# Reordering the last two heads, and moving small transposes and loads, in a hybrid decoder layer on one Trainium2 core

## The chip, the cores and the metric

The kernel runs on one core of one Trainium2 chip. A core has a matrix engine (TensorE: PE in the profile, PEld for its weight loads), VectorE (DVE), ScalarE (ACT), GpSimd (POOL) and SyncE (SP, whose queue issues most DMAs). Each engine executes its own instructions in order and waits on semaphores for the others. The metric is the device time of one execution in microseconds.

## The reference

One layer of a decoder over 2048 prompt positions of width 1024, and one new position for each of 8 sample rows with 512 positions of paged cache behind them. All arrays are float32.

```python
h = rms_norm(x, g_norm); p = h @ w_in            # 1024 -> 3592
q, k, v, fz, za, u, gv, zc = split(p)            # 8 heads x 64; 4 groups x 128
q, k = rms_norm(q, g_q), rms_norm(k, g_k)        # per head
c = cumsum(log_sigmoid(fz + b_f))
s[t, s'] = q_t . k_s' * 64**-0.5 + c_t - c_s'    # causal
attn = softmax(s) @ v
mix = tril(w_s) @ rms_norm(gv) + b_s             # in chunks of 128 positions
y = x + concat(attn * silu(za), u * mix * silu(zc)) @ w_out
```

The sample rows do the same, with keys, values and forget values of their cache pages in front. Outputs are y, k, v and the log forget values for both, and the normalised gv of the sample rows.

## The kernel before

Float32 products are made of parts: an operand is split into a high part and a remainder (`split`: ScalarE or GpSimd writes the high part, VectorE subtracts), and the projections add three matmuls (high by high, high by low, low by high).

The work has three stages.

*First stage (to about 585 us).* `order` goes through eight units of input columns. Units 3, 0, 1, 2 (q, k, v, fz) and 4 (gv) run over the 16 token tiles; units 5, 6 (u, zc) and 7 (za) run by features over the first two of four 512-token chunks. `load_unit` loads the next unit's eight weight tiles through three `raw` buffers and splits them. `sample_products` (helper lines 412, 413 copy its result out) makes a unit's product for the 8 sample rows, in a PSUM bank of the same four (`acc`) in the gv unit; it stands ahead of token tile 14. Results go to DRAM scratch (`qk_hi`, `qk_lo`, `v_st`, `mixT`, `zT`).

*Second stage (to about 1150 us).* `UNITS` lists pairs (head, chunk of 512 queries). For each, `values(at)` runs over key tiles of 128: two score matmuls into a `sc` bank, ScalarE's exp into `p` (L1036; a ring of ten), GpSimd's running sum `acc` of p for the row sums (L1043, L1045), and p times v into the `av` bank in groups of eight. Scores are shifted by each query's extreme score, which `maxima` finds beforehand with one rougher matmul into `tp` banks (three) and reductions on VectorE (L970, L972, L983); a transpose and a copy (L991) bring it into a row (`shifts`), stored to `mrow`, and `load_queries` loads queries and shift together. The maxima run ahead of the attention by `AHEAD` of a head, head after head. `load_head` loads a head's keys for the maxima (`k2`), keys for the scores (`k1`) and values, a piece every `LSTEP`.

At the end of a unit, L1057 and L1058 copy the result to `at`, which goes to `aT` in DRAM; `add_up` transposes `acc`, sums it (L1066) and takes the reciprocal (L1067); `done` transposes that, and L1073 copies it to a row stored in `rT`. After each odd head's chunk, `gate` loads the pair's 128 rows of z (`zT`), a (`aT`) and r (`rT`, spread over partitions), multiplies z by r on GpSimd (L1133) and that by a on VectorE (L1134), and stores `gm`.

The remaining two chunks of u, zc and za are the `filler`: matmuls into one bank (`fl`) that `fill` puts between the attention's, in proportion to `FILL`, `FILL0` (first chunk of a head) or `FILL7` (the last units). When it is used up, the out weights are loaded and split (`load_out_weights`, L1114, L271) and the out tiles follow as filler, if their inputs are there. The sample rows' gating and attention (`decode_gate`, `decode_attention`) are spread over the stage from head 1 on; L718 is a prefix sum on VectorE.

*Third stage.* The out tiles that are left: 16 tiles of 128 tokens, two halves of 512 columns (`out_products`), added to x and stored.

TensorE's order is the program's own. Its clock `Pe.clock` is counted by hand in ns of matmul work; `later(ns, fn)` puts off a piece of work by so much TensorE work, and what is so given is not issued ahead of TensorE's latest matmul at that place. So the constants (`SLAG`, `STLAG`, `GTLAG`, `OLAG`, `FGAP` and so on) are distances in TensorE work. The other engines' order is the scheduler's, within these bounds. SBUF tiles of 512 columns rotate through 11 buffers (`wk`), those of 2048 through 16.

Of the kernel before, what the change touches and what calls it, by code (L numbers as in the profile page):

```python
# [9 lines left out]
F32 = mybir.dt.float32  # L10
# [4 lines left out]
ALU = mybir.AluOpType  # L15
# [4 lines left out]
P = 128  # L20
# [4 lines left out]
NH = 8  # L25
# [15 lines left out]
WOLAG = 9000.0  # L41
WOSTEP = 1500.0
OLAG = 9000.0
GTLAG = 8000.0
STLAG = 5000.0
STLAST = 2500.0
SLAG = 3000.0
# [5 lines left out]
FGAP = 1500.0  # L53
# [7 lines left out]
VPARTS = 7  # L61
QLEAD = 10
PRE = 1.2
DEC = (3300, 15000, 26000, 14000)
# [4 lines left out]
WOENG = ('act',)  # L69
# [15 lines left out]
def hymba_step(ctx, tc, x_prompt, x_sample, cache_k, cache_v, cache_logf, page_table, g_norm, w_in,  # L85
# [615 lines left out]
    def decode_attention():  # L701
# [16 lines left out]
        nc.vector.tensor_tensor_scan(cc, one, lfT, 0.0, op0=ALU.mult, op1=ALU.add)  # L718
# [23 lines left out]
        for b in range(B):  # L742
            hs = slice(b * NH, (b + 1) * NH)
            vb = s8(t="vb").rearrange("p (g f) -> p g f", g=NPG)
            page_loads(b, range(NPG), [(cv, lambda g: vb[:, g])])
# [12 lines left out]
            yield DEC[2]  # L758
# [114 lines left out]
    def load_head(h):  # L873
# [24 lines left out]
        return [lambda: keys(0), rows_of, lambda: keys(1)], [  # L898
# [43 lines left out]
    def maxima(hd):  # L942

        h = hd["h"]
        nxt = qhi.pop() if qhi else load_hi(h, 0)
        for c in range(2):
            q = nxt
            for i in range(8 * c, 8 * c + 8, 2):
                if i == 2:
                    nxt = load_hi(h, 1)  # L950
                if i == 10 and h + 1 < NH:
                    qhi.append(load_hi(h + 1, 0))
                if i % 4 == 0:
                    part = sm.tile([P, 4, i // 4 + 1], F32, tag="mn", bufs=3, name=tname("mn"))
                cuts = [pieces((j + 1) * P) for j in (i, i + 1)]
                ends = []
                for j, cut in zip((i, i + 1), (cuts[0], cuts[1][::-1])):
                    for (c0, m) in cut:
                        n = cuts[j - i].index((c0, m))
                        end = n == len(cut) - 1  # L960
                        sp = bank("tp")[:, :m]
                        mm(sp, q[:HD + 2, (j % 8) * P:(j % 8 + 1) * P], hd["k2"][:HD + 2, c0:c0 + m], True, not end,
                           max(m, 256) * 0.422)
                        if end:
                            ends.append((sp, m, j, n))
                            if j > i:
                                for (sp, m_, _, _) in ends:
                                    mm(sp[:, m_ - P:], identb, maskb[:, 0], False, True, 56)
                                for (sp, _, j_, n_) in ends:
                                    nc.vector.tensor_reduce(part[:, j_ % 4, n_:n_ + 1], sp, axis=AX.X, op=ALU.min)  # L970
                        else:
                            nc.vector.tensor_reduce(part[:, j % 4, n:n + 1], sp, axis=AX.X, op=ALU.min)  # L972
                        yield m * 0.422
                if i % 4 == 2:
                    shifts(h, i // 4, part)

    shifted = set()
    qhi = []
# [19 lines left out]

    avq = []
# [13 lines left out]
    def values(at):  # L1013
# [3 lines left out]
        for kt in range(4 * c + 4):  # L1017
            if kt == 1 and c == 0 and h < NH - 1:
                Pe.loads += chain(*load_head(h + 1))
                Pe.load_at = Pe.clock + LHEAD  # L1020
            if at + 1 < len(UNITS) and UNITS[at + 1] not in qload and kt >= 4 * c + 4 - (
                    QLEAD if UNITS[at + 1] in shifted else 4):
                qload[UNITS[at + 1]] = load_queries(*UNITS[at + 1])
# [23 lines left out]
            def step(kt=kt, p=p, n0=n0, acc=acc, c=c, st=st, at=at):  # L1047
# [7 lines left out]
                if fin:  # L1055
                    t = s2(t="at")
# [4 lines left out]
                    def add_up():  # L1061
# [7 lines left out]
                        def done():  # L1069
# [5 lines left out]
                            def store():  # L1075
                                nc.sync.dma_start(rT[h, c * 512:(c + 1) * 512].rearrange("(n p) -> n p", p=P), t)
                                if h % 2:
                                    later(STLAST, lambda: gate(h // 2, c))
# [304 lines left out]
```

## Time and profile before

| | |
|---|---|
| runs of the kernel | 1331.54, 1327.94, 1326.21 us; median 1327.94 |
| the profiled execution | 1326.85 us, span 1325.0 us, mean granted TensorE clock 0.992 |
| TensorE busy | 97% of the span, 6544 matmuls |
| VectorE, ScalarE, GpSimd busy | 49%, 33%, 42% |
| DMA | 201 MB, mean 152 GB/s |

Times in the profile are microseconds from the span's start. A line such as `PE tp L200 <- DVE sm L1067: 4.1, 3, 2.0` says that TensorE's instructions of line 200 that write `tp` waited 4.1 us in all, three times, 2.0 at most, and that the last thing they waited for was the VectorE instruction of line 1067 that writes `sm`. A helper's instructions all have the helper's line: 196 is any matmul, 200 any transpose. A timeline row has start, duration, engine, line, operation and tiles, shapes, count, and in brackets the engine's idle time before it and what ended it. Matmuls are pipelined: a busy TensorE can still be slowed by a lower clock, which the table of stretches shows as granted clock.

### The profile page before, as it was taken

To read this page: it belongs to the slowest core of one execution; us is meant where nothing else is said; L and a number is where in the kernel's file an instruction comes from. 1 tells how busy PE (TensorE), PEld (TensorE's weight loads), DVE (VectorE), ACT (ScalarE), POOL (GpSimd) and SP (SyncE) were. 2 spreads that over 40 slices of the span, in tenths; PEclk is the share of its full clock that TensorE was granted. 3 is DMA by queue.
4 is the path that set the end of the run, shared out by engine and by line. 5 is a ranking of instruction groups with operands and counts; after the bars stand their busy time and mean duration, and the time that the engine had idled before them with its cause. 6 is when DMAs were issued, how large, how long until landed. Compare 5 with 4: busy or idle time off the path is not lost.

```text
span 1325.0 us, 19322 instructions
## 1 busy us (share of the span) xinstructions
PE 1289.8 (97%) x6544; PEld 1005.7 (76%) x6544; DVE 646.6 (49%) x1216; ACT 432.1 (33%) x781; POOL 559.0 (42%) x587
## 2 busy tenths in 40 slices
PE   6999999999999999999999999999999999999998
PEld 5999999999888777866666666666656565788877
DVE  4445654534667643354476544454444566322321
ACT  5542332222222111114444444444444556300100
POOL 3113343322222555305656566566656759600000
PEclk9999999999999999999999999999999999999999
DMA  6644353555213868945436584576464545773221
GB/s 220 186 121 116 89 139 113 150 144 144 81 46 81 289 209 278 290 137 137 103 85 172 158 211 123 149 221 181 131 181 128 153 132 181 200 264 116 96 81 48
DMA packets 189028, 201.43 MB, mean 152 GB/s; under 512 B 40002, under 2 KB 138626, under 8 KB 188906
## 3 DMA queue, kind: packets, MB, share of 16 engines
q1 hardware_dynamic: 185042, 191.43, 50.5%
q10 hardware_dynamic: 3488, 8.39, 1.6%
q8 instruction: 52, 0.85, 0.3%
q14 instruction: 46, 0.38, 0.1%
q0 software_dynamic: 400, 0.38, 0.1%
HBM read 127.43 MB, written 72.73 MB: 151 GB/s over the span
## 4 chain that ended last, share of the span: by engine, by line
PE 90%; DVE 3%; DMA 2%; issue 2%; ACT 1%; POOL 1%; SPq 1%; DVEq 0%; POOLq 0%; ACTq 0%
PE acc L196 36%; PE sc L196 22%; PE fl L196 10%; PE av L196 9%; PE tp L196 6%; PE tp L200 4%; PE pm L196 3%; DMA xp<-in_x_prompt_dram 1%; DMA q<-qk_hi 1%; POOL acc L1045 0%; DMA g<-gm 0%; ACT p L1036 0%; SPq L326 0%; DVE wl L279 0%; DVE mn L972 0%
## 5 line engine op out<-in xcount | busy, mean ns | idle before, releaser
L1045 POOL TENSOR_TENSOR acc<-acc,p 128x512 f32<-128x512 f32 (+3 forms) x256 | 287.8, 1124 | 79.7 <-ACT p L1036 64.3
L1036 ACT ACTIVATE p<-sc,zero 128x512 f32<-128x512 f32 (+1 forms) x320 | 194.8, 623 | 177.3 <-PE sc L196 166.7
L196 PE MATMUL acc<-wh,hh 128*128 128x384 f32 (+2 forms) x640 | 229.0, 358 | 0.0
L196 PE MATMUL acc<-wl,hh 128*128 128x384 f32 (+2 forms) x640 | 223.3, 349 | 1.2 <-DVE wl L279 1.2
L196 PE MATMUL acc<-wh,hl 128*128 128x384 f32 (+2 forms) x640 | 223.0, 348 | 0.6 <-DVE hl L271 0.6
L196 PE MATMUL sc<-q,k 128*128 128x512 f32 (+7 forms) x640 | 202.4, 397 | 2.2 <-DMA q<-qk_hi 1.5
L196 PE MATMUL sc<-wo,am 128*128 128x512 f32 x720 | 164.1, 390 | 0.0
L196 PEld LDWEIGHTS sc<-wo,am 128*128 128x128 f32 x720 | 135.0, 188 | 28.2
L972 DVE TENSOR_REDUCE mn<-tp 128x1 f32<-128x320 f32 (+5 forms) x192 | 119.3, 633 | 73.7 <-PE tp L196 72.7
L196 PE MATMUL av<-p,vst 128*64 128x512 f32 (+3 forms) x640 | 135.0, 542 | 0.0
L196 PEld LDWEIGHTS sc<-q,k 128*128 128x128 f32 (+1 forms) x640 | 119.1, 197 | 18.8 <-ACT p L1036 3.6
L196 PEld LDWEIGHTS acc<-wh,hh 128*128 128x128 f32 x640 | 120.8, 189 | 7.0 <-ACT hh L266 0.2
L196 PEld LDWEIGHTS acc<-wl,hh 128*128 128x128 f32 x640 | 121.0, 189 | 6.8 <-DVE wl L279 2.3
L196 PEld LDWEIGHTS acc<-wh,hl 128*128 128x128 f32 x640 | 120.5, 188 | 6.2 <-DVE hl L271 1.1
L196 PE MATMUL tp<-k,q 66*128 66x384 f32 (+6 forms) x320 | 121.4, 393 | 3.3 <-DVE mx L983 1.1
L259 POOL TENSOR_SCALAR sm<-sm 128x6 f32<-128x6 f32 (+3 forms) x84 | 19.9, 237 | 242.8 <-DVE sm L424 174.5
L196 PEld LDWEIGHTS av<-p,vst 128*64 128x64 f32 x640 | 47.8, 137 | 67.0 <-issue 58.3
L970 DVE TENSOR_REDUCE mn<-tp 128x1 f32<-128x512 f32 (+7 forms) x128 | 66.8, 563 | 59.9 <-PE tp L196 59.7
L260 POOL TENSOR_TENSOR sm<-sm,mhalf 128x6 f32<-128x6 f32 (+3 forms) x84 | 89.5, 1066 | 6.7
L1043 POOL TENSOR_TENSOR acc<-p 128x512 f32<-128x512 f32 x32 | 41.6, 1300 | 104.7 <-ACT p L1036 91.6
L196 PEld LDWEIGHTS tp<-k,q 66*128 66x128 f32 x320 | 61.1, 192 | 29.8 <-issue 5.9
L1171 DVE TENSOR_TENSOR xy<-xy,sc 128x512 f32<-128x512 f32 x30 | 20.6, 687 | 119.8 <-PE sc L196 119.8
(213 smaller groups left out, 1899.4 us busy)
## 6 DMA issues: line engine op xcount, KB each, us to landing
kb<-in_cache_k_dram SPq DMA_DIRECT2D x32, 256.0 KB
k<-qk_hi SPq DMA_DIRECT2D x32, 256.0 KB
q<-qk_hi SPq DMA_DIRECT2D x64, 128.0 KB
vb<-in_cache_v_dram SPq DMA_DIRECT2D x32, 256.0 KB
g<-gm SPq DMA_DIRECT2D x16, 512.0 KB
xy<-in_x_prompt_dram SPq DMA_DIRECT2D x16, 512.0 KB
out_dram<-xy ACTq DMA_DIRECT2D x15, 512.0 KB
xp<-in_x_prompt_dram SPq DMA_DIRECT2D x12, 512.0 KB
```

The lines of the kernel that those rows point to most:

```text
L196: Pe.last = nc.tensor.matmul(out, lhsT, rhs, start=start, stop=stop).ins
L200: Pe.last = nc.tensor.transpose(out, in_, idn).ins
L259: nc.gpsimd.tensor_scalar(r, ss, inv_n, EPS, op0=ALU.mult, op1=ALU.add)
L260: nc.gpsimd.tensor_tensor(r, r, mhalf[:rows, :n], op=ALU.pow)
L970: nc.vector.tensor_reduce(part[:, j_ % 4, n_:n_ + 1], sp, axis=AX.X, op=ALU.min)
L972: nc.vector.tensor_reduce(part[:, j % 4, n:n + 1], sp, axis=AX.X, op=ALU.min)
L1036: nc.scalar.activation(p[:, n0:], sp[:, n0:], AF.Exp, bias=zero1, scale=-1.0)
L1043: nc.gpsimd.tensor_tensor(acc, p0, p, op=ALU.add)
L1045: nc.gpsimd.tensor_tensor(acc[:, n0:], acc[:, n0:], p[:, n0:], op=ALU.add)
L1171: nc.vector.tensor_tensor(xy[:, fs], xy[:, fs], po, op=ALU.add)
```

## The change

- `sample_products` of the gv unit stands ahead of tile 11 (`SAT`).
- The maxima follow `UNITS` a chunk at a time (not head after head), and in `UNITS` head 7's chunks start one place earlier, between those of head 6. Head 7's keys for the maxima are loaded from head 5's third chunk on, in front of the list of loads; its other pieces from head 6's first chunk on.
- The first unit's queries are loaded as soon as its shift is stored.
- The sample rows' prefix sum is made in four pieces; their value pages are loaded one by one and in half the time.
- For odd heads the attention result stays on chip: it is put into the upper half of the gate's tile `ga`, and the gate's other inputs (`gate_inputs`) are loaded when the row sums are ready, except the odd head's own row.
- Transposes of row sums come 4000 ns of TensorE work after the sums (`RSLAG`, before 2000), those of maxima after 4500 (`SLAG`, before 3000). Other distances change as listed.
- Out weights are loaded three at a time, and the first two out tiles run as first halves, then second halves; a half needs only its own half of the out weights. The last four units (before, three) use `FILL7`.

```diff
-WOLAG = 9000.0
+WOLAG = 5000.0
-GTLAG = 8000.0
+GTLAG = 4000.0
+OLAG0 = 5000.0
+RTLAG = 1500.0
+NDENSE = 4
-SLAG = 3000.0
+SLAG = 4500.0
+SAT = 11
+RSLAG = 4000.0
-FGAP = 1500.0
+FGAP = 2500.0
-UNITS = [(h, c) for h in range(6) for c in range(4)] + [(6, 0), (6, 1), (6, 2), (7, 0), (6, 3), (7, 1), (7, 2), (7, 3)]
+UNITS = [(h, c) for h in range(6) for c in range(4)] + [(6, 0), (6, 1), (7, 0), (6, 2), (7, 1), (6, 3), (7, 2), (7, 3)]
-LSTEP = 3000.0
+LSTEP = 2200.0
-DEC = (3300, 15000, 26000, 14000)
+DEC = (3300, 15000, 13000, 12000)
...
-        nc.vector.tensor_tensor_scan(cc, one, lfT, 0.0, op0=ALU.mult, op1=ALU.add)
+        for g in range(NPG):
+            gs_ = slice(g * P, (g + 1) * P)
+            nc.vector.tensor_tensor_scan(cc[:, gs_], one[:, gs_], lfT[:, gs_], cc[:, g * P - 1:g * P] if g else 0.0,
+                                         op0=ALU.mult, op1=ALU.add)
+            yield 1500
...
-            page_loads(b, range(NPG), [(cv, lambda g: vb[:, g])])
+            for g in range(NPG):
+                page_loads(b, (g,), [(cv, lambda g: vb[:, g])])
+                if g < NPG - 1:
+                    yield DEC[2] / NPG
...
-            if kt == 1 and c == 0 and h < NH - 1:
-                Pe.loads += chain(*load_head(h + 1))
+            if kt == 1 and (c == 0 and h < NH - 2 or (h, c) == (NH - 3, 2)):
+                parts = load_head(len(heads))
+                if c == 0:
+                    Pe.loads += chain(*parts)
+                else:
+                    Pe.loads[:0] = parts[0]
+                parts_of[0] = parts[1]
                 Pe.load_at = Pe.clock + LHEAD
+            if kt == 1 and (h, c) == (NH - 2, 0):
+                Pe.loads += parts_of[0]
...
-                    t = s2(t="at")
-                    nc.scalar.copy(t[:HD], av[HD:])
-                    nc.vector.tensor_tensor(t[:HD], t[:HD], av[:HD], op=ALU.add)
-                    later(STLAG if h < NH - 2 else STLAST, lambda: nc.sync.dma_start(aT[h * HD:(h + 1) * HD, c * 512:(c + 1) * 512], t[:HD]))
+                    if h % 2 == 0:
+                        t = s2(t="at")
+                        nc.scalar.copy(t[:HD], av[HD:])
+                        nc.vector.tensor_tensor(t[:HD], t[:HD], av[:HD], op=ALU.add)
+                        later(STLAG, lambda: nc.sync.dma_start(aT[h * HD:(h + 1) * HD, c * 512:(c + 1) * 512], t[:HD]))
+                    else:
+                        t = s2(t="ga")
+                        nc.scalar.copy(t[HD:], av[:HD])
+                        nc.vector.tensor_tensor(t[HD:], t[HD:], av[HD:], op=ALU.add)
...
+                            ins_ = gate_inputs(h // 2, c, t) if h % 2 else None
...
-                                    later(STLAST, lambda: gate(h // 2, c))
-                            later(STLAG if h < NH - 2 else STLAST, store)
-                        later(2000, done)
+                                    later(STLAST, lambda: gate(h // 2, c, *ins_))
+                            later(STLAG if h < NH - 2 else RTLAG, store)
+                        later(RSLAG, done)
...
-        for h in range(NH):
-            while h not in heads or "k2" not in heads[h] or h and len(Pe.loads) > VPARTS:
-                if not Pe.loads:
-                    raise RuntimeError(h)
+        for (h, c) in UNITS:
+            while h not in heads or "keys" not in heads[h]:
                 load_next()
-            yield from maxima(heads[h])
+            yield from maxima(h, c)
...
+                if n + 3 < KT:
+                    load(n + 3, KORDER[n + 3])
             later(WOLAG, parts)
-        for n, k in enumerate(KORDER):
-            later(n * WOSTEP, lambda n=n, k=k: load(n, k))
+        for n in range(3):
+            later(n * WOSTEP, lambda n=n: load(n, KORDER[n]))
...
+    def gate_inputs(k, c, a):
+        z, r = s2(t="gz"), s2(t="gr")
+        cs = slice(c * 512, (c + 1) * 512)
+        nc.sync.dma_start(z, cols_of(zT, k, c))
+        nc.sync.dma_start(a[:HD], aT[2 * k * HD:(2 * k + 1) * HD, cs])
+        nc.sync.dma_start(r[:HD], rT[2 * k, cs].partition_broadcast(HD))
+        return a, z, r
+
+    def gate(k, c, a, z, r):
+        nc.sync.dma_start(r[HD:], rT[2 * k + 1, c * 512:(c + 1) * 512].partition_broadcast(HD))
...
-        later(OLAG, parts)
+        later(OLAG if i >= OFIRST else OLAG0, parts)
...
-        for i in range(NT):
-            while i not in ins or not ins[i] or len(wo_hl) < 2 * KT:
+        halves = [(0, 0), (1, 0), (0, 1), (1, 1)] + [(i, f) for i in range(2, NT) for f in range(2)]
+        for n, (i, f) in enumerate(halves):
+            while i not in ins or not ins[i] or (KORDER[-1], f) not in wo_hl:
...
-                    if i == NT - 2:
+                    if i == (NT - 2 if u < 4 else SAT):
                         group.insert(0, sample_products(unit, WID[u], SEGS[u], "acc" if u == 4 else "pm"))
...
-        dose = FILL7 if at >= len(UNITS) - 3 else FILL0 if c == 0 else FILL
+        dose = FILL7 if at >= len(UNITS) - NDENSE else FILL0 if c == 0 else FILL
```

More of the change, by code (lines that the diff above doesn't have):

```diff
@@ L940, in load_hi @@
         return t
[L942 to L975, printed above, removed]
@@ new lines, in hymba_step, with maxima @@
+    HALVES = list(dict.fromkeys((h, c // 2) for h, c in UNITS))
+    def maxima(h, c):
+        hd, at = heads[h], HALVES.index((h, c // 2))
+        for half in HALVES[:1] if at == 0 else ():
+            if half not in qhi:
+                qhi[half] = load_hi(*half)
+        q = qhi[h, c // 2]
+        part = sm.tile([P, 4, c + 1], F32, tag="mn", bufs=3, name=tname("mn"))
+        for i in range(4 * c, 4 * c + 4, 2):
+            if i % 4 == 2 and at + 1 < len(HALVES) and HALVES[at + 1] not in qhi:
+                qhi[HALVES[at + 1]] = load_hi(*HALVES[at + 1])
+            cuts = [pieces((j + 1) * P) for j in (i, i + 1)]
+            ends = []
+            for j, cut in zip((i, i + 1), (cuts[0], cuts[1][::-1])):
+                for (c0, m) in cut:
+                    n = cuts[j - i].index((c0, m))
+                    end = n == len(cut) - 1
+                    sp = bank("tp")[:, :m]
+                    mm(sp, q[:HD + 2, (j % 8) * P:(j % 8 + 1) * P], hd["k2"][:HD + 2, c0:c0 + m], True, not end,
+                       max(m, 256) * 0.422)
+                    if end:
+                        ends.append((sp, m, j, n))
+                        if j > i:
+                            for (sp, m_, _, _) in ends:
+                                mm(sp[:, m_ - P:], identb, maskb[:, 0], False, True, 56)
+                            for (sp, _, j_, n_) in ends:
+                                nc.vector.tensor_reduce(part[:, j_ % 4, n_:n_ + 1], sp, axis=AX.X, op=ALU.min)
+                    else:
+                        nc.vector.tensor_reduce(part[:, j % 4, n:n + 1], sp, axis=AX.X, op=ALU.min)
+                    yield m * 0.422
+        shifts(h, c, part)
@@ L1196, in out_tiles @@
                     yield -1
-            for n in range(1, OAHEAD + 1):
-                prepare(i + n)
-            if i == 8:
+            for j in range(2 if n < 4 else i + 1, n + 1 if n < 4 else i + OAHEAD + 1):
+                prepare(j)
+            if (i, f) == (8, 0):
                 for _ in Pe.steps:
@@ L1204, in out_tiles @@
                 gs = decode_out()
-            if gs is not None and i < 12:
+            if gs is not None and i < 12 and f == 0:
                 next(gs, None)
-            yield from out_products(i, **ins.pop(i), tags=("sc", "sc") if last_phase[0] else ("fl", "fl"))
+            yield from out_products(i, f, **ins[i], tag="sc" if last_phase[0] else "fl")
     mgen = all_maxima()
@@ L1319, in hymba_step @@
         pump()
-    qload[UNITS[0]] = load_queries(*UNITS[0])
+        if UNITS[0] in shifted and UNITS[0] not in qload:
+            qload[UNITS[0]] = load_queries(*UNITS[0])
+    if UNITS[0] not in qload:
+        qload[UNITS[0]] = load_queries(*UNITS[0])
     vdone = 0.0
```

52 lines of the change are left out of this document (23 added, 29 removed).

## The prediction

> **What bounds the kernel now.** The page comes first: TensorE is busy nearly all the time and the chain that ended last is TensorE.
>
> ```profile
> span 1325.0 us, 19322 instructions
> PE 1289.8 (97%) x6544; PEld 1005.7 (76%) x6544; DVE 646.6 (49%) x1216; ACT 432.1 (33%) x781; POOL 559.0 (42%) x587
> PE 90%; DVE 3%; DMA 2%; issue 2%; ACT 1%; POOL 1%; SPq 1%; DVEq 0%; POOLq 0%; ACTq 0%
> ```
>
> The change neither adds nor removes a matmul (all 6544 stay, in another order), so it can only win or lose time in which TensorE stands or runs at a lower clock. The list of what TensorE waited for names the standing, and a table of busy time by stretch names the clock (columns: stretch, PE, PEld, DVE, ACT, POOL, granted clock, DMA share, GB/s).
>
> ```profile
> PE tp L200 <- DVE xp L343: 10.0, 1, 10.0
> PE tp L200 <- DVE sm L1067: 4.1, 3, 2.0
> PE tp L200 <- DVE mx L983: 2.4, 1, 2.4
> PE acc L196 <- DVE s L413: 2.4, 1, 2.4
> PE sc L196 <- DMA q<-qk_hi: 1.5, 1, 1.5
> PE fl L196 <- DVE sz L525: 1.5, 1, 1.5
> PE tp L200 <- DVE mn L970: 1.5, 1, 1.5
> PE tp L196 <- DVE mx L983: 1.1, 1, 1.1
> PE sc L196 <- ACT p L1036: 0.7, 2, 0.4
> PE tp L200 <- ACT ob L753: 0.6, 1, 0.6
> PE tp L196 <- DVE mn L970: 0.5, 2, 0.3
> ```
>
> ```profile
> 437.70:441.10 3.40, 3.40 (x10) 2.64 (x9) 2.47 (x5) 1.34 (x2) 2.58 (x4) 0.50 0.89 321
> 690.20:697.20 7.00, 6.78 (x21) 4.98 (x22) 2.40 (x7) 2.08 (x5) 1.74 (x2) 0.51 0.35 97
> 717.60:721.00 3.40, 3.40 (x10) 2.63 (x9) 2.74 (x7) 0.95 (x2) 1.67 (x2) 0.50 0.71 218
> 1075.90:1079.50 3.60, 3.60 (x10) 1.59 (x11) 2.18 (x6) 2.57 (x6) 3.42 (x3) 0.53 0.65 203
> 1120.30:1123.80 3.50, 3.50 (x9) 2.82 (x10) 3.50 (x4) 2.23 (x5) 3.34 (x4) 0.51 0.43 146
> 725.00:960.00 235.00, 234.78 (x1202) 151.96 (x1200) 113.64 (x205) 102.95 (x186) 147.01 (x135) 1.00 0.62 168
> 1100.00:1150.00 50.00, 47.29 (x221) 28.82 (x220) 26.09 (x28) 29.02 (x52) 44.96 (x35) 0.97 0.63 189
> 1150.00:1320.00 170.00, 170.00 (x756) 137.98 (x755) 44.17 (x55) 14.13 (x16) 2.29 (x2) 1.00 0.38 129
> ```
>
> The first wait (10.0) is the start and stays. The other ten make 16.3 us. Five stretches run at half clock and lose half of themselves: 1.7, 3.4, 1.7, 1.7, 1.7, together 10.2 us. So all that the change can touch is 26.5 us. The output projection (1150 to 1320) has TensorE busy in all of its 170.00 us: nothing to win there, whatever order its halves take.
>
> **The change part by part.** The profiled execution took 1326.85 us (span 1325.0 and 1.85 around it), 1.1 below the median of the three runs shown, 1327.94. The sum is made on 1326.85.
>
> (a) The sample rows' product of the gv unit moves from tile 14 to tile 11 (SAT). TensorE now waits 2.40 us for its PSUM bank, and a half-clock stretch follows.
>
> ```profile
> 436.34 0.51 PE L196 MATMUL acc<-hh,wh 128*128 128x512 f32 x1 [2.40 <-DVE s L413]
> 443.64 0.70 POOL L278 TENSOR_SCALAR wh<-raw,gT 128x512 fp32r<-128x512 f32 x1 [3.11 <-DMA raw<-in_w_in_dram]
> 444.38 0.75 DVE L279 SCALAR_TENSOR_TENSOR wl<-raw,gT,wh 128x512 fp32r<-128x512 f32 x1 [1.04 <-POOL wh L278]
> 445.15 0.39 PE L196 MATMUL acc<-hl,wh 128*128 128x512 f32 x1
> ```
>
> Moved, that bank is long free, worth 2.4 + 1.7 = 4.1. But see what is late next: the last of the next unit's eight weight tiles is split at 444.38 + 0.75 = 445.13, and its first user, the matmul one step (0.23) after the one at 445.15, runs at 445.38, with 0.25 us to spare. Run 4.1 us earlier, TensorE meets that tile 3.85 us too soon if the tile's load (three raw buffers, a DMA that POOL waited 3.11 for) does not move. Bounds: 4.1 gained, or 1.5 lost (4.1 - 3.85 - another 1.7 of half clock). I take 1.5 gained, near the middle, since the splits ahead of the tile no longer share DVE with the sample's copy out.
>
> (b) The first unit's queries are loaded as soon as their shift is known, not after the first stretch of maxima: the wait of 1.5 for q goes; the keys behind it were loaded long before. 1.5 (0 to 1.5).
>
> (c) The transposes of sums come later (RSLAG, 2000 to 4000 ns of TensorE work). Three waits on L1067, and the one credited to the maximum (L983) at 690, are this transpose standing in front of DVE's in-order queue:
>
> ```profile
> 676.32 4.26 DVE L430 TENSOR_TENSOR nrm<-ps,sm 8x512 f32<-8x512 f32 x1 [0.33 <-POOL sm L260]
> 688.32 0.67 DVE L1066 TENSOR_REDUCE sm<-tp 128x4 f32<-128x512 f32 x1
> 690.42 0.37 PE L200 MATMUL tp<-ident,sm 128*4 128x128 f32 x1 [2.40 <-DVE mx L983]
> 1075.38 0.27 PE L200 MATMUL tp<-ident,sm 128*4 128x128 f32 x1 [1.73 <-DVE sm L1067]
> 1120.27 0.33 PE L200 MATMUL tp<-ident,sm 128*4 128x128 f32 x1 [1.99 <-DVE sm L1067]
> ```
>
> At 690 DVE is behind from the sample's gating (one operation of 4.26). 2.0 us more work covers 2.0 of 2.4; what is late next is the PSUM bank that L1066 still holds for the following maxima, about 0.5 more. So 2.4 + 3.4 - 0.9 = 4.9 (2.4 to 5.8). The three on L1067 (0.36, 1.73, 1.99) are all within 2.0: 4.1 + 1.7 + 1.7 = 7.5 (3 to 7.5).
>
> (d) The sample attention's scan is cut in four, 1500 ns apart, and the maxima's transposes come 1.5 us later (SLAG).
>
> ```profile
> 715.47 1.43 DVE L718 TENSOR_TENSOR_SCAN cc<-one,lfT 64x512 f32<-64x512 f32 x1 [1.89 <-ACT lfT L717]
> 717.40 0.27 PE L200 MATMUL tp<-ident,mx 128*4 128x128 f32 x1 [1.46 <-DVE mn L970]
> ```
>
> Four pieces hold the same columns; with an overhead that I put at a quarter of the whole they cost DVE 1.8 instead of 1.43, but none blocks for more than 0.45: 1.5 + 1.7 - 0.2 = 3.0 (0 to 3.2). The waits of 1.1, 0.6 and 0.5 on maxima and the sample's output copy shrink with SLAG too: 1.2 of 2.2.
>
> (e) FGAP (1500 to 2500) lets the filler's only bank empty: 1.0 of the 1.5 on L525. (0 to 1.5)
>
> (f) New order of the last two heads, maxima in that order, head 7's keys first, out-weights in threes, out halves, NDENSE: the same work. POOL's sum of a 512-wide p takes 1.319 us, and in 1100:1150, where little filler is left, POOL is busy 44.96 of 50.
>
> ```profile
> L1045 POOL TENSOR_TENSOR acc<-acc,p 128x512 f32<-128x512 f32 x168 | 221.6, 1319 | 69.7 <-ACT p L1036 60.4 <-ACT rows L1073 0.4
> ```
>
> More filler there (halves that need only the first half of the out-weights, and tile inputs whose lags are shorter) keeps TensorE from running into POOL: the waits on p (0.7) may go. I count nothing, since the other waits of that stretch are in (c). If the cover is missing (the first outputs still late), 0.7 stays and POOL has no room for a delay. Head 7's keys take four places in SP's queue a unit and a half sooner; queries are issued ten steps ahead of use there, which covers it, and without that cover the price is another wait like the 1.5 in (b).
>
> (g) The sample's value pages come in half the time (DEC: 13 instead of 26 us for four pages), issued singly on SP: the same 32 loads.
>
> ```profile
> vb<-in_cache_v_dram SPq DMA_DIRECT2D x32, 256.0 KB
> L677 SPq DMA_DIRECT2D vb<-in_cache_v_dram x32: 332/342/381, 755.4 to 972.3; - x32
> 500.00:525.00 25.00, 25.00 (x112) 20.12 (x111) 9.17 (x14) 2.10 (x3) 12.89 (x11) 1.00 0.91 274
> ```
>
> That is 8.4 MB in about 108 us rather than 217, some 39 GB/s on top of the 168 of 725 to 960, or a DMA share of 0.62 x 207 / 168 = 0.76. With 0.91, from 500 to 525, TensorE did not stand at all. Nothing counted (0 to 2 lost, a wait like that in (b)).
>
> (h) Odd heads gated on chip.
>
> ```profile
> L1130 SPq DMA_DIRECT2D gr<-rT x32: 450/462/1339, 709.3 to 1155.5; - x32
>   DVE ga L1134: 20.1, 7
> ```
>
> Sixteen stores of aT go; each of the 16 gates still issues four loads, but z, a and one r come at the row sums, and only one r at the gate itself, while GTLAG falls from 8000 to 4000. So POOL's product z*r comes 4.0 us sooner after a gate that issues three loads fewer (about 0.46 each, 1.4): 2.6 us less room for that DMA. Behind POOL's product stand the sums of p, whose ring ScalarE's exps wait for; behind DVE's L1134 the maxima, whose three banks TensorE waits for. DVE waited 20.1 us in seven gates already (row above) without one TensorE wait named after it. The tile `ga` is also held from the unit's end to its store, about 12 + 4 + 5 + 2.5 + 4 + 5 = 33 us instead of two holds of about 5 and 13, out of 11 buffers. Bounds: 0, or 16 x 2.6 = 42 us if every bit of DVE's delay reached TensorE. The row is near 0; I take 3. For maxima that now meet DVE's backlog in the place of the moved transposes, 2, and 1 for buffers.
>
> Sum: gains 1.5 + 1.5 + 4.9 + 7.5 + 3.0 + 1.2 + 1.0 = 20.6, losses 6, net 14.6: 1326.85 - 14.6 = 1312.3, and on the runs' median 1.1 more, **1313 us**, 1.1% less.
>
> [...] In the trace the waits of 2.4, 2.4, 1.5, 1.7 and 2.0 us each have a half-clock stretch of some 3.4 or 7 us beginning within 1.4 us of their end, and the 1.5 on q and on L525 have none. [...]
>
> **The rivals.** One more stretch of the table bears on the second of them.
>
> ```profile
> 680.00:725.00 45.00, 40.91 (x182) 26.80 (x180) 29.61 (x53) 19.08 (x37) 27.85 (x24) 0.89 0.53 147
> ```
>
> 1. All waits go and nothing comes: 26.5 less the 2.6 kept in (a) is 23.9, so 1304. For it: 725:960 stands 0.22 us in 235, so this schedule can be that dense. Against: (h).
> 2. The waits only move: DVE's backlog is the cause, and the next maxima matmul meets it. Then (c) and (d) save 5 of 16.6 with the losses unchanged: the net is 20.6 - 11.6 - 6 = 3.0 and the time 1325, no change. For it: DVE is busy 29.61 of 45 us around the waits at 690 and 717 (row above). Against: it catches up, since after 725 TensorE hardly stands.
>
> 3. The clock falls for another reason than these waits, at times of its own: the 8.5 us of clock in (c) and (d) stay lost, 1313 + 8.5 = 1321.5, at the edge of no change. Against: each of the five stretches has its wait. [...]
> 4. Slower: late r. POOL's product waits for the one load, DVE behind it, and TensorE with them at every gate. It decides when a gate costs TensorE more than (20.6 - 3) / 16 = 1.1 us; at the full 2.6, 42 - 17.6 = 24 us more, 1352; at 2 us, 32 - 17.6 = 14, 1342. Against: seven gates with 20.1 us of DVE waiting cost nothing.
>
> **How the numbers follow.** Forecast 0.48, rivals 0.17, 0.17, 0.05, 0.13. One half per cent of 1327.94 is 6.6 us, about what a measurement here can tell from no change: faster ends at 1321.3, slower begins at 1334.6. Faster: 0.48 + 0.17 and a share of the third, 0.67; same 0.20; slower 0.13. The range goes from 2 below the first rival (a little more than the sum's 26.5) past the second and third; it leaves out most of the fourth and the ends of the others, under 0.2: 1302 to 1332. The forecast's own, by the bounds of (a) to (h), is 1306 to 1320.
>
> **What would show it.** (a) no wait on L413, a small one on L279 or L278 near 440. (c) L1067 gone from TensorE's waits, three half-clock stretches gone (about 690, 1075, 1120). (d) none near 717. (f) filler at 1100, `wo` before 1131, and the projection dense to the end. (h) no TensorE wait behind L1134 or POOL; if DVE's waits on `gz` go well above 20.1 and TensorE's waits on `tp` with them, the fourth is right. New half-clock stretches anywhere make the prediction wrong first.

## The result and the profile after

The changed kernel takes 1334.6 us in the median, the kernel before 1327.8 beside it: ratio 1.0042, 95% interval 1.0022 to 1.0061, some 6 us slower. That is still within the half per cent that the prediction took as the limit of no change, but the interval lies above 1. The medians, here and in the table below, count every execution, also a few far slower ones (one of the changed kernel's eight took 2110.8 us; without it the median is 1333.9), which the ratios leave out. The prediction said 1313, with a range of 1302 to 1332. The profiled execution of the changed kernel took 1332.3 us (span 1330.6, mean granted clock 0.990), and it is this one that is read below. The edit shifts the line numbers: 199 is any matmul, 203 any transpose, 1053 the exp, 1088 the sum, 1160 and 1161 the gate's products on GpSimd and VectorE.

The page shows the same matmuls and nearly the same busy time as before on every engine:

```profile
span 1330.6 us, 19269 instructions
PE 1294.4 (97%) x6544; PEld 1006.1 (76%) x6544; DVE 647.3 (49%) x1219; ACT 434.3 (33%) x781; POOL 556.6 (42%) x587
```

What TensorE waited for, in the changed kernel (the rows that are spoken of; some of 1.1 us and less are left out):

```profile
PE tp L203 <- DVE xp L346: 9.9, 1, 9.9
PE tp L199 <- DVE mn L982: 4.2, 6, 1.6
PE tp L199 <- DVE sm L1088: 3.2, 4, 1.3
PE tp L199 <- DMA k<-qk_hi: 2.0, 1, 2.0
PE sc L199 <- DMA q<-qk_hi: 1.7, 2, 1.2
PE tp L203 <- DVE fz_all L483: 1.6, 1, 1.6
PE fl L199 <- DVE am L274: 1.1, 1, 1.1
PE fl L199 <- ACT am L269: 1.0, 1, 1.0
PE tp L203 <- DVE mn L980: 0.8, 1, 0.8
```

The transposes (203) of the second stage are nearly gone from this list, as intended: nothing waits for the sum L1088 at a transpose any more, and one wait of 0.8 is left (that on `fz_all` stands at 23 us, in the first stage). In their place stand matmuls of line 199 into the same `tp` banks, that is, maxima, behind the same VectorE work; and three waits of the second stage that before had not: head 7's keys, and twice an out tile's input (`am`). The stretches at half clock (columns as before; the seventh figure is the granted clock):

```profile
687.30:690.70 3.40, 3.40 (x11) 2.41 (x12) 1.30 (x3) 0.94 (x3) 1.28 (x1) 0.50 0.65 163
875.00:878.40 3.40, 3.40 (x12) 2.20 (x10) 0.78 (x3) 0.69 (x1) 3.17 (x4) 0.50 0.52 143
994.50:1001.40 6.90, 6.90 (x23) 4.34 (x23) 1.92 (x4) 2.69 (x5) 3.40 (x4) 0.51 0.90 215
1066.20:1069.60 3.40, 3.40 (x10) 0.89 (x11) 1.81 (x3) 2.05 (x4) 2.54 (x2) 0.50 0.82 224
1096.90:1103.70 6.80, 6.25 (x15) 4.95 (x16) 5.99 (x6) 3.96 (x6) 6.56 (x4) 0.50 0.31 108
```

The one at 437 is gone and the first score matmul comes 3.9 us sooner than before (592.6 for 596.4). The second stage then gives back 9.4: TensorE's gaps of over 0.15 us between 596 and 1200 add up to 16.2 us (before 13.2), the half clock there costs 11.9 (before 8.5), and about 3 us show as no wait.

Three places show how. At the gate, the chain of waits of the changed kernel (start, duration, what) runs from the odd head's row to TensorE:

```profile
865.73 5.20 DMA gr<-rT
871.05 1.29 POOL gz L1160
872.36 1.75 DVE ga L1161
874.67 0.78 PE tp L199 x2
```

This is the path of the prediction's fourth rival: GpSimd waits for the row, VectorE for GpSimd, and two maxima matmuls 1.56 us for VectorE; the clock falls at 875.0. Head 7's keys (timeline rows):

```profile
979.21 0.44 SPq L893 DMA_DIRECT2D k<-qk_hi  x1
988.80 0.45 SPq L893 DMA_DIRECT2D k<-qk_hi  x1
990.40 0.45 SPq L949 DMA_DIRECT2D q<-qk_hi  x1
993.37 0.47 PE L199 MATMUL tp<-k,q 66*128 66x128 f32 x2 [1.96 <-DMA k<-qk_hi]
```

The second half of the keys is issued 4.6 us ahead of its first use, and eleven other DMAs of SP's queue stand between the two halves. And the first out tile:

```profile
1094.57 1.04 ACT L269 CAST am<-g 128x1024 fp32r<-128x1024 f32 x1 [0.45 <-DMA g<-gm]
1095.66 0.73 PE L199 MATMUL fl<-wo,am 128*128 128x512 f32 x2 [1.03 <-ACT am L269]
1096.18 1.22 DVE L274 TENSOR_TENSOR am<-g,am 128x1024 fp32r<-128x1024 f32 x1
1097.45 0.80 PE L199 MATMUL fl<-wo,am 128*128 128x512 f32 x1 [1.06 <-DVE am L274]
```

The product is given out before its input is split, high part and remainder alike.

### The profile page after: what moved, and what is told of

It reads as the page before. It is cut to its first block, busy times and chain, and to the rows that moved or that the text cites. A ratio compares the mean times of both kernels' runs of the same rounds, so it can differ in the third digit from the quotient of the medians.

```text
span 1330.6 us, 19269 instructions
## 1 busy us (share of the span) xinstructions
PE 1294.4 (97%) x6544; PEld 1006.1 (76%) x6544; DVE 647.3 (49%) x1219; ACT 434.3 (33%) x781; POOL 556.6 (42%) x587
## 4 chain that ended last, share of the span: by engine, by line
PE 88%; DMA 4%; DVE 3%; issue 1%; SPq 1%; ACT 1%; POOL 1%; POOLq 0%; DVEq 0%; ACTq 0%
PE acc L199 36%; PE sc L199 20%; PE fl L199 12%; PE av L199 8%; PE tp L199 6%; PE tp L203 4%; PE pm L199 3%; DMA xp<-in_x_prompt_dram 1%; DMA q<-qk_hi 1%; DMA gr<-rT 1%; DVE mn L982 1%; POOL acc L1062 1%; DMA raw<-in_w_out_dram 0%; DMA vst<-v_st 0%; SPq L329 0%
## 5 line engine op out<-in xcount | busy, mean ns | idle before, releaser
L1062 POOL TENSOR_TENSOR acc<-acc,p 128x512 f32<-128x512 f32 (+3 forms) x256 | 284.4, 1111 | 98.2 <-ACT p L1053 82.8
L199 PE MATMUL sc<-q,k 67*128 67x512 f32 (+7 forms) x640 | 202.7, 395 | 1.8 <-DMA q<-qk_hi 1.7
L199 PE MATMUL sc<-wo,am 128*128 128x512 f32 x600 | 136.9, 390 | 0.0
L199 PEld LDWEIGHTS sc<-wo,am 128*128 128x128 f32 x600 | 112.4, 188 | 23.5
L262 POOL TENSOR_SCALAR sm<-sm 128x6 f32<-128x6 f32 (+3 forms) x84 | 20.1, 239 | 239.0 <-DVE sm L427 170.0
L263 POOL TENSOR_TENSOR sm<-sm,mhalf 128x6 f32<-128x6 f32 (+3 forms) x84 | 89.8, 1070 | 6.7
L199 PE MATMUL acc<-hh,wh 128*128 128x512 f32 x192 | 75.1, 391 | 0.0
```

The costliest lines, as they stand in the source:

```text
L199: Pe.last = nc.tensor.matmul(out, lhsT, rhs, start=start, stop=stop).ins
L262: nc.gpsimd.tensor_scalar(r, ss, inv_n, EPS, op0=ALU.mult, op1=ALU.add)
L263: nc.gpsimd.tensor_tensor(r, r, mhalf[:rows, :n], op=ALU.pow)
L1062: nc.gpsimd.tensor_tensor(acc[:, n0:], acc[:, n0:], p[:, n0:], op=ALU.add)
```

## The experiments

All kernels were timed against the kernel before. "Clock lost" is the span times one less the mean granted clock, "rest" the span times the clock, both medians over the runs; the first is what half-clock stretches cost, the second is work and waits. The kernel before had 10.6 to 11.9 and 1314.9 to 1316.9 beside the experiments.

| kernel | median us | ratio to before (95%) | clock lost | rest |
|---|---|---|---|---|
| the changed kernel | 1334.6 | 1.0042 (1.0022 to 1.0061) | 13.3 | 1319.5 |
| e1_sat: before, product at tile 11 | 1324.5 | 0.9965 (0.9950 to 0.9981) | 7.9 | 1313.6 |
| e2_gate_lag: changed, GTLAG 8000 | 1327.2 | 0.9994 (0.9978 to 1.0010) | 9.3 | 1315.9 |
| e3_first_tiles: changed, OLAG0 9000 | 1331.8 | 1.0031 (1.0015 to 1.0048) | 10.6 | 1320.9 |
| e4_pages: changed, pages in fours | 1333.5 | 1.0044 (1.0027 to 1.0060) | 16.0 | 1317.1 |
| e5_small_parts: before, (a) to (e) | 1338.6 | 1.0076 (1.0048 to 1.0104) | 22.0 | 1314.8 |
| e6_keys_early: changed, keys sooner | 1328.4 | 1.0007 (0.9990 to 1.0025) | 9.3 | 1318.0 |
| e7_old_order: changed, old `UNITS` | 1323.1 | 0.9961 (0.9939 to 0.9982) | 7.9 | 1313.3 |
| e8_repair: e2, e3 and e6 together | 1329.1 | 1.0000 (0.9983 to 1.0016) | 10.6 | 1316.7 |
| e9_sums_later: e1 and RSLAG | 1327.2 | 0.9987 (0.9973 to 1.0000) | 8.6 | 1316.2 |
| e10_maxima_later: e1, SLAG, scan | 1338.7 | 1.0075 (1.0057 to 1.0094) | 20.1 | 1316.8 |
| e11_queries_fgap: e1, (b), (e) | 1324.2 | 0.9967 (0.9953 to 0.9980) | 9.3 | 1311.9 |
| e12_order_gate: e7 and GTLAG 8000 | 1320.8 | 0.9933 (0.9914 to 0.9952) | 6.6 | 1312.2 |
| e13_sums_back: e12, RSLAG 2000 | 1319.3 | 0.9926 (0.9900 to 0.9953) | 9.9 | 1308.6 |
| e14_maxima_back: e12, SLAG 3000 | 1319.2 | 0.9932 (0.9911 to 0.9954) | 4.0 | 1313.5 |
| e15_ahead: e10, AHEAD 0.75 | 1326.7 | 0.9972 (0.9951 to 0.9994) | 9.3 | 1316.5 |
| e16_tiles_later: e12, OLAG0 9000 | 1323.0 | 0.9955 (0.9932 to 0.9977) | 7.9 | 1313.7 |

**The sample product alone, on the kernel before** (`SAT` as in the change).

```diff
-                    if i == NT - 2:
+                    if i == (NT - 2 if u < 4 else SAT):
```

> The kernel before with one part of the change alone: the sample rows' product of the gv unit ahead of tile 11 instead of 14. Theory A (each part of the change has its own price, and this one is a plain gain): the wait of 2.4 us on L413 near 434 and the half-clock stretch of 3.4 us behind it go, nothing else moves; 4.1 us less, about 1324 against 1328. Theory B (a removed wait comes back at the next late thing, as the prediction had it for the weights): a wait of 1 to 4 us on the split weights near 440, and between 2 us less and 1 us more.

4.6 us less. The wait of 2.4 and its half clock are gone, and TensorE waits for none of the next weights, feared late, so their loads and splits did not stay where they were. The two gaps that are there (0.27 at 427, 0.56 at 447) are for other operands, the split of gv and a bank that VectorE still reads. The stretch is at full clock:

```profile
426.00:447.00 21.00, 20.36 (x98) 16.78 (x97) 18.68 (x36) 5.27 (x8) 8.54 (x10) 1.00 0.84 264
```

**Three single repairs of the changed kernel.** The gates' distance, the first out tiles' distance, and the value pages.

```diff
-GTLAG = 4000.0
+GTLAG = 8000.0
```

> The changed kernel with the gates' lag put back (GTLAG 8000 instead of 4000). Theory A (GpSimd's product waits for the late row of r, VectorE behind it, TensorE behind that): the waits near 721 (1.3 us) and 873 (1.6 us and 3.4 us at half clock) go, GpSimd's 11.1 us of waiting on gr falls below 3; 3 to 5 us less than the changed kernel. Theory B (VectorE is late anyway, the wait moves to the next matmul that needs a tp bank): waits on tp stay at 12 us or more in the second stage and the time within 2 us of the changed kernel's.

```diff
-OLAG0 = 5000.0
+OLAG0 = 9000.0
```

> The changed kernel with the first two out tiles' lag put back (OLAG0 9000 instead of 5000). Theory A (the first out products are issued before their input is split): the two waits on am near 1095 (1.0 and 1.1 us) and the 6.8 us at half clock behind them go; 4 to 5.5 us less than the changed kernel. Theory B: the filler that comes 4 us later leaves a hole in which other waits appear; within 2 us of the changed kernel.

```diff
-            for g in range(NPG):
-                page_loads(b, (g,), [(cv, lambda g: vb[:, g])])
-                if g < NPG - 1:
-                    yield DEC[2] / NPG
+            page_loads(b, range(NPG), [(cv, lambda g: vb[:, g])])
...
-            yield DEC[2] / NPG
+            yield DEC[2]
```

> The changed kernel with the sample rows' four value pages of a row issued together again, at the new pace of a row in 13 us. Theory A (single page loads stand in SP's queue in front of the queries): the wait of 1.2 us for q near 850 goes, 1 to 2 us less. Theory B (SP's queue is blocked by what it waits for anyway): the wait for q stays or comes at another unit, within 1 us.

The gates are worth 0.0048 of the time, 6 us: the waits at 721 and 873 go (VectorE waits for `gz` 6.7 us in place of 13.6). The out tiles are worth 0.0011, within the intervals: their waits move from 1095 to 1106 and 1113. The pages are worth nothing: the query that waited 1.15 at 850 is on time, and another waits 1.94 at 776.

**The small parts alone, on the kernel before.** SAT, the early first queries, RSLAG, SLAG, the scan in four and FGAP as in the change; units, gates and loads as before.

```diff
-                        later(2000, done)
+                        later(4000, done)
...
-SLAG = 3000.0
+SLAG = 4500.0
-FGAP = 1500.0
+FGAP = 2500.0
```

> The kernel before with the small parts of the change alone: the gv unit's sample product at tile 11, the first queries as soon as their shift is stored, transposes of sums and maxima later (4000 and 4500 ns), the prefix sum in four pieces, FGAP 2500. Old order of the last heads, old gate, old loads. Theory A (what is transposed later is no longer waited for, as the prediction has it): 4.6 for the sample product (measured alone) + 1.5 + 4.9 + 7.5 + 4.2 + 1.0 = 23.7 less, about 1304 to 1308 us, no half-clock stretch near 690, 717, 1076, 1120. Theory B (VectorE is late there and the next maxima meet it): 4.6 + 1.5 + about 5, so 1316 to 1320 us; waits of about 1.2 us on tp<-k,q near 684 and 1118, each with its half-clock stretch; none near 1076.

Neither: 0.0111 more than the product alone, all of it clock (22.0 lost, the rest as low as before's). Both theories fell here, and the parts were taken singly below.

**Head 7's keys, the order, and three repairs together.**

```diff
-            if kt == 1 and (c == 0 and h < NH - 2 or (h, c) == (NH - 3, 2)):
+            if kt == 1 and (c == 0 and h < NH - 2 or (h, c) == (NH - 3, 1)):
```

> The changed kernel, with head 7's keys called for from head 5's second chunk on (one chunk earlier). Theory A (the wait of 1.96 us at 991 is these keys, which land 1 to 5 us ahead of their first use): that wait and its 6.8 us at half clock go, 5.4 us less, about 1329 us. Theory B (VectorE's and SP's backlog at that place is the cause, or the keys only push out another load): a wait of over 1 us within 30 us of 991 stays, with clock, 1332 to 1336 us.

```diff
-... + [(6, 0), (6, 1), (7, 0), (6, 2), (7, 1), (6, 3), (7, 2), (7, 3)]
+... + [(6, 0), (6, 1), (6, 2), (7, 0), (6, 3), (7, 1), (7, 2), (7, 3)]
```

> The changed kernel with the order of units of before (head 7 starts one place later); all else stays. Theory A (the order is what loses: head 7's keys late, and its maxima, gates and out-weight splits together between 1055 and 1070): the wait at 991 and the four between 1059 and 1066 go with their clock, about 5.4 + 2.8 + 1.7 = 10 us less, 1323 to 1327 us. Theory B (the gates' late rows and the first out tiles lose, whatever the order): waits near 721, 873 and 1095 stay as they were, and 1331 to 1336 us.

> The changed kernel with three things mended together: gates 8000 ns after the row (GTLAG), the first two out tiles' inputs split after 9000 ns (OLAG0), head 7's keys one chunk earlier. Theory A (each loss is its own and they add up): 6 (gates, measured alone) + 1.5 (first tiles, measured alone) + 5.4 (keys) less than 1334.6, about 1321 to 1323 us. Theory B (they stand in one VectorE backlog, and what one stops losing the next loses): no less than with the gates alone, 1327 to 1330 us.

With the keys asked for a chunk sooner, the wait at 991 and its stretch are gone and 988 to 1000 runs at full clock (a wait of 0.98 for another piece of keys stands at 970, without half clock behind it):

```profile
988.00:1000.00 12.00, 11.64 (x66) 7.87 (x63) 6.75 (x12) 5.76 (x12) 7.61 (x8) 1.00 0.93 220
```

0.0035, close to the 5.4 us expected. The old order is worth 0.0081, 11 us, the most of any single repair. Between 1040 and 1130 the changed kernel first, the old order second:

```profile
1040.00:1130.00 90.00, 84.83 (x392) 54.81 (x392) 55.54 (x84) 43.62 (x80) 55.65 (x47) 0.94 0.53 157
L199 PE MATMUL tp<-k,q x39: 334/395/575, 1040.4 to 1121.0; 66*128 66x512 f32 x15, 66*128 66x480 f32 x8, 66*128 66x448 f32 x7, 66*128 66x384 f32 x4
```

```profile
1040.00:1130.00 90.00, 87.86 (x428) 57.25 (x425) 55.76 (x83) 51.58 (x92) 66.52 (x57) 0.98 0.48 152
L199 PE MATMUL tp<-k,q x37: 284/393/507, 1041.7 to 1096.2; 66*128 66x512 f32 x14, 66*128 66x384 f32 x6, 66*128 66x448 f32 x6, 66*128 66x416 f32 x4
```

In the same 90 us the old order gets 428 matmul records through, the new one 392 (not quite the same mix of work). In the new one maxima last to 1121, into the out tiles' splits that are then due; in the old one they end at 1096, before the first tile's split at 1101. In 1059 to 1070 and 1094 to 1104 VectorE of the changed kernel has little room; the old order's rows for the same times stand below:

```profile
1059.00:1070.00 11.00, 8.17 (x30) 3.68 (x30) 9.41 (x17) 6.16 (x11) 8.25 (x6) 0.84 0.52 147
1094.00:1104.00 10.00, 7.91 (x22) 5.64 (x21) 9.16 (x10) 6.29 (x10) 7.49 (x4) 0.66 0.51 194
```

```profile
1059.00:1070.00 11.00, 10.28 (x54) 7.26 (x53) 8.92 (x16) 7.66 (x14) 4.21 (x5) 1.00 0.65 196
1094.00:1104.00 10.00, 8.63 (x40) 4.93 (x40) 7.87 (x12) 6.57 (x12) 9.61 (x9) 0.83 0.76 265
```

The busy share does not tell the two orders apart: VectorE has as much to do over the 90 us (55.5 and 55.8) and nearly as much in the first of the short stretches (9.41 and 8.92). What differs is the bunching. In the new order VectorE works from 1054.8 to 1066.7 without a pause (a gate's product, splits of out weights, sums, maxima); in the old one it pauses five times between 1055 and 1068, 4.1 us in all, and no gate's product falls there. No run changes the bunching alone, so that it is what costs the time there is argued, not shown.

The wait at 991 and the four between 1059 and 1066 go but for one of 0.7, as the first theory had it; the gates' waits at 721 and 873 stay, as the second had it for those places. The two for `am` near 1095 go as well, against the second theory, and a maximum waits 1.41 there instead. The three repairs together bring 0.0042, less than the gates alone: their single gains do not add up (0.0094 singly). In that kernel a wait of 2.5 us stands at 1058 and one of 3.6 at 1103.

**The small parts one at a time, on the kernel before with SAT; and the two best repairs together.** For the first, only `later(4000, done)`; for the second, SLAG 4500 and the scan in four; for the third, the first queries and FGAP; the fourth is the changed kernel with the old `UNITS` and GTLAG 8000.

> The kernel before with the sample product at tile 11 and, of the other small parts, only the later transposes of row sums (4000 for 2000 ns). All small parts together took 1338.6 us and lost 22 us of clock (span times one less the granted clock; before 10.6). Theory A (as predicted in (c)): 4.6 for the product and 12.4 for the transposes, about 1311 to 1313 us. Theory B (the waits only move, one for one): 4.6 less and nothing more, 1322 to 1326 us. Theory C (these later transposes are what cost the small parts their clock): 1332 to 1338 us, over 18 us of clock lost.

> The kernel before with the sample product at tile 11 and, of the other small parts, only the later transposes of maxima (4500 for 3000 ns) and the prefix sum in four pieces. Theory A (as predicted in (d)): 4.6 and 4.2, about 1319 to 1321 us. Theory B (waits move): 1322 to 1326 us. Theory C (the later shifts make the queries late and cost the clock): 1332 to 1338 us, waits on sc<-q,k, over 18 us of clock lost.

> The kernel before with the sample product at tile 11 and, of the other small parts, only the first queries as soon as their shift is stored and FGAP 2500. Theory A (as predicted in (b) and (e)): 4.6 and 2.5, about 1321 to 1323 us, clock lost as in the product alone (7.9). Theory B (no effect of its own): 1323 to 1326 us. Theory C (these cost the clock): 1332 to 1338 us.

> The changed kernel with the old order of units (1323.1 us alone) and gates 8000 ns after the row instead of 4000 (7 us less in the new order). Theory A (late rows at the gates cost the same whatever the order): 1316 to 1318 us; waits near 721 and 873 gone with their clock. Theory B (with the old order the gates' delay is hidden at the end, so half or less is left to win): 1320 to 1324 us.

Later sums: no gain, rather 0.0022 more than the product alone, at the edge of what the intervals can tell. Its waits and timeline rows show them moved to the maxima:

```profile
PE tp L197 <- ACT rows L1074: 2.8, 4, 1.8
PE tp L197 <- DVE mn L973: 2.7, 3, 2.1
PE sc L197 <- ACT p L1037: 1.8, 2, 1.5
PE tp L197 <- DVE sm L1067: 1.1, 1, 1.1
```

```profile
869.57 0.27 PE L201 MATMUL tp<-ident,sm 128*4 128x128 f32 x1
869.81 1.74 DVE L1135 SCALAR_TENSOR_TENSOR ga<-ga,gz 128x512 f32<-128x512 f32 x1 [1.89 <-POOL gz L1134]
872.11 0.46 PE L197 MATMUL tp<-k,q 66*128 66x416 f32 x1 [2.07 <-DVE mn L973]
...
1078.72 0.27 PE L201 MATMUL tp<-ident,sm 128*4 128x128 f32 x1
1081.99 0.25 ACT L1074 COPY rows<-tp 4x128 f32<-4x128 f32 x1
1082.30 0.74 PE L197 MATMUL tp<-k,q 66*128 66x448 f32 x1 [1.84 <-ACT rows L1074]
```

The transpose runs without a wait, but its result then sits in a `tp` bank until ScalarE copies it out (3.3 us later at 1078, behind casts of out weights that wait for their loads), or VectorE is held by a gate; the next maximum finds no bank.

Later maxima are where the clock went. Windows of that kernel, then of the kernel before:

```profile
1053.60:1063.40 9.80, 8.72 (x26) 4.51 (x24) 8.84 (x18) 0.52 (x2) 2.33 (x2) 0.75 0.52 149
1058.50:1072.20 13.70, 13.13 (x38) 7.82 (x38) 7.91 (x15) 2.95 (x7) 3.44 (x4) 0.50 0.42 118
1130.20:1140.40 10.20, 8.84 (x18) 3.25 (x20) 9.44 (x7) 7.71 (x13) 9.94 (x7) 0.50 0.60 164
```

```profile
1053.60:1063.40 9.80, 9.80 (x56) 6.60 (x53) 4.67 (x8) 4.88 (x10) 7.72 (x9) 1.00 0.73 181
```

For 9.8 us TensorE does 26 matmuls and not 56, ScalarE has two instructions, VectorE is busy 8.84. The timeline shows why: almost nothing but maxima, each paced by a reduction of 0.6 us (three of TensorE's rows):

```profile
1055.17 2.56 PE L197 MATMUL tp<-k,q 66*128 66x512 f32 x5
1057.89 0.50 PE L197 MATMUL tp<-k,q 66*128 66x512 f32 x1 [0.16 <-DVE mn L977]
1059.09 4.07 PE L197 MATMUL tp<-k,q 66*128 66x512 f32 x7 [0.57 <-DVE mn L977]
```

The code gives the row: `load_queries` runs maxima until its unit's shift has been given out, and that is now put off by 4500 ns of TensorE work, which only maxima can supply. Attention stands meanwhile. Whether the stretch near 1130 follows from that is open: e15 below, without the row, has 10.2 us at half clock at 1119.3.

The first queries and FGAP have no effect of their own that shows (0.9967 against 0.9965), though the waits they aimed at fall (q 0.15, L526 gone). Old order and long gate distance together give 0.9933: of the 6 us that the gates cost in the new order about 4 are still there to win in the old (0.9961 to 0.9933, the intervals overlap). The time lies in the second theory's range, but the waits near 721 and 873 go, as the first had it, and 4 of 6 is more than half.

**What was left open.** Whether the row of maxima is the whole of the 14 us, and whether the transposes matter at all in the best kernel so far, e12 (the changed kernel with the old order and gates at 8000).

```diff
-RSLAG = 4000.0
+RSLAG = 2000.0
```

> The changed kernel with the old order of units and gates 8000 ns after the row (1320.8 us), and now the transposes of row sums back at 2000 ns. Theory A (as predicted in (c), the later transposes save their waits): these come back, 12 us more, 1331 to 1334 us. Theory B (a late VectorE costs TensorE the same wherever it meets it): 1319 to 1323 us; waits of 2 us or more on tp<-ident,sm near 686 in place of 1.3 on tp<-k,q. Theory C (the later transposes themselves lose 2 to 3 us, as they did on the kernel before): 1317 to 1319 us.

```diff
-SLAG = 4500.0
+SLAG = 3000.0
```

> The same kernel (1320.8 us) with the transposes of maxima back at 3000 ns, those of sums at 4000. Theory A (as predicted in (d), 1.2 from this part): 1322 us. Theory B (no effect: the later shift costs only where a unit's queries have to force the maxima through, which this kernel's maxima, in the order of the units, never do): 1319 to 1323 us. Theory C (the later shift costs 14 us of clock in any kernel, as it did on the kernel before): 1307 to 1312 us.

```diff
-AHEAD = 0.65
+AHEAD = 0.75
```

> The kernel before with the sample product at tile 11, transposes of maxima at 4500 ns, the prefix sum in four (1338.7 us so far), and the maxima now 0.75 of a head ahead of the attention (AHEAD, 0.65). Theory A (the 14 us come from one place near 1054, where a unit's queries wait for a shift that is put off by 4500 ns of TensorE work and 17 maxima are forced through in one row at VectorE's pace, after which ScalarE is late): with the maxima further ahead there is no such row, 1322 to 1327 us, 8 to 11 us of clock lost. Theory B (transposes of maxima at 4500 ns are late for the queries everywhere): 1334 to 1340 us, over 18 us of clock lost.

> The changed kernel with the old order of units and gates 8000 ns after the row (1320.8 us), and the first two out tiles' inputs split 9000 ns after their load (OLAG0, 5000). Theory A (the two waits near 1110 are products given out before their input is split): those go with their 3.4 us at half clock, 1316 to 1318 us. Theory B (splits come when VectorE and ScalarE have time, not when they are given out, and the next product meets them): 1319 to 1323 us.

Sums back and maxima back each leave the time where it was (0.9926 and 0.9932 against 0.9933). With the sums back the old pair of waits is there again, 2.5 at a transpose near 684 for 1.3 at a maximum, its list of waits has

```profile
PE tp L203 <- DVE mx L992: 2.5, 1, 2.5
```

and the time is the same. With the maxima further ahead the forced row is gone and so are 12 of the 14 us (0.9972 against 1.0075), so the later shift costs where it makes the queries wait for the maxima, not everywhere. That the row alone costs all of it is not shown: its own stretch at half clock loses 6.8 us, half-clock stretches near 686, 871 and 963 went as well, and the longer lead was not run with the shift at 3000. Splitting the first out tiles later wins nothing: the waits near 1110 are gone and one of 3.58 for a unit's queries stands at 1113.

The old order, gates at 8000 and either transpose (1319 to 1321 us) beat both kernels; the three versions can't be told apart. Which of the parts that stayed in them (odd heads gated on chip, halves of out tiles, out weights in threes, loads) makes the 4 us by which e12 beats the product alone was not run.

## Why the prediction was wrong

Two steps failed: that a transpose put off saves the wait for VectorE's backlog ((c), and the transposes' part of (d)), which measured nothing or a loss, and that the new order is "the same work" at no cost ((f)), which measured 11 us.

(a), taken as 1.5 from bounds of 4.1 and -1.5, measured 4.6. What failed is the bound "does not move": the next unit's weights did not stay behind the product, and no wait for them came.

(b) and (e), 1.5 and 1.0: the waits fell as said, the time did not measurably (1324.2 against 1324.5).

(c), 12.4, is the largest gain that failed to come. The waits were read rightly, VectorE's backlog in front of the sum, but "2.0 us more work covers 2.0 of 2.4", with only 0.5 held back for the bank, failed. Alone it cost 2.7 us on the kernel before (at the edge of the noise), and in the changed kernel with the old order and gates at 8000, taking it back changed nothing. A wait of VectorE or ScalarE that the transpose no longer meets is met by the next maximum, which needs one of the same three banks. This was the second rival's claim, and its figure for the change's gains was the nearer one.

(d), 4.2: the scan's wait at 716 went, though the scan's 3.0 was not run alone; its four pieces took 0.48, 0.48, 0.87 and 0.86 us in the changed kernel, 2.69 together for the 1.43 of the whole before, not 0.45 each (the overhead of a quarter was the author's estimate). But SLAG, credited with 1.2, costs (with the scan) 14 us on the kernel before, where head follows head, for the most part where it forces the row. In e12, whose maxima follow the units as the change's do, SLAG is worth nothing either way.

(f), counted at zero, is the other failure and the largest loss: 11 us. "queries are issued ten steps ahead of use there, which covers it" named the wrong transfer: it was the keys themselves that came late (1.96 and 3.4 of clock; 4.6 us measured by the early keys), and the rest of the waits that the old order removes lies between 1059 and 1104, where maxima, a gate and splits now meet on VectorE (argued from the trace, as said above). The work was the same, its place was not. The projection stayed dense, and filler did come sooner, at 1096, but with inputs not yet split.

(g), zero, held.

(h), 6, was about right in size (GTLAG alone, 6) and its path was right: of the two waits that the odd row makes, the one at 873 goes through GpSimd, VectorE and `tp` to TensorE exactly as the fourth rival had it. But the sign it named, VectorE's wait on `gz` well above 20.1, did not come: it fell to 13.6. GpSimd's wait on `gr` is what rose, from 2.5 to 26.4 (one of 15.3 among them). A total over gates does not tell whether the one that matters is there.

So the second rival had the fate of (c), and the fourth a path that cost 6 us, with waits at two gates and not at every one; none of the four had the loss of the new order. Put together as if they added, the measured effects (4.6 gained, 11 and 6 lost) make 12 us slower, and about 6 were measured. The single effects do not add (the three repairs together gave less than half of their sum), so no exact ledger closes the 21.6 us between 1313 and 1334.6. The 26.5 us that "the change can touch" left out eight shorter rows of the same list, 4.7 us; nothing above hangs on them.

## What to carry to other kernels

When a wait ends on a shared engine that is behind, giving the waiting instruction more room can just hand the wait to the next user of the same buffers, as here (in the second stage TensorE waited 8.0 us for VectorE's reductions at transposes before, and 7.7 at maxima after); ask which work that engine does late, and move that. A reorder is not free just because its work is the same: list, for each piece moved forward, when its transfers are issued, and count the engines' work in the stretch it lands in. Where code forces work until a delayed step is given out, a longer delay can turn into a row of that work.

## What had not been expected of the hardware

The prediction took about 1.5 us as the shortest wait that costs clock (1.46, at 717 in the kernel before, was the shortest with a half-clock stretch behind it). Here a wait of 1.23 us at 684.4 has a stretch at half clock from 687.3 on, while one of 1.34 at 721.0 has none:

```profile
685.64 0.39 PE L199 MATMUL tp<-k,q 66*128 66x256 f32 x1 [1.23 <-DVE sm L1088]
717.00:725.00 8.00, 6.66 (x36) 4.43 (x33) 4.03 (x8) 1.19 (x2) 3.47 (x4) 1.00 0.52 148
```

And during the row of maxima of e10 the granted clock is 0.50 for 13.7 us, from 1058.5 on, with no wait above 0.57: in the 9.8 us from 1053.6 TensorE does 26 matmuls (the kernel before 56) and stands for 1.08 us in all. So the length of a wait alone does not settle it. The half-clock stretches listed for the changed kernel, e10 and e15 are 3.4, 6.8 to 6.9, 10.2 and 13.7 us long, one to four times about 3.41.

The traces show when the clock changes, too. In the changed kernel it changes at 687.29, 690.70, 875.02, 878.44, 994.49, 1001.31, 1066.17, 1069.58, 1096.89 and 1103.72, all whole multiples of 3.4133 us apart (416.43 from the first to the last, 122 of them). The ten changes of the kernel before, from 437.70 to 1123.78, are so as well (686.08, 201 of them). Steps of this length can be counted off from them. The wait from 684.42 to 685.64 lies whole in the step from 683.88 to 687.29. The one from 720.96 to 722.30 is cut by the bound at 721.42 into 0.46 and 0.88. In these two traces, between 100 and 1310 us, seven steps at full clock have TensorE standing for 1.69 us or more in sum, and half clock follows all seven. Of the seven with 1.11 to 1.56 it follows three, those with 1.31, 1.52 and 1.56, and not those with 1.11, 1.14, 1.28 and 1.50. Of the 680 with less, at most 0.88, it follows none. So in these two traces the sum of the standing in one step tells more than the length of a wait, and where a wait falls matters as well. What decides between 1.11 and 1.56, and what lowers the clock in e10's row of maxima, was not shown.

From run to run the changed kernel lost 9.3 to 16.0 us of clock, while its rest stayed within 1317.3 to 1320.6: most of its scatter is the clock's.
